# Two PSUM tiles in place of one two-bank tile for the transposes, and VectorE in place of GpSimd from attention slot 20

## The chip, the cores and the metric

The kernel runs on one core of one Trainium2 chip. The metric is the device time of one execution in microseconds (us); less is better. Five engines have instruction streams of their own: PE (TensorE), DVE (VectorE), ACT (ScalarE), POOL (GpSimd) and SP, which here only issues transfers. Each engine carries out its stream in order and waits on semaphores that other engines or transfers raise.

## The reference

One decoder layer on 512 tokens of width 1024, in float32:

```python
h = rmsnorm(x, g_mix_pre[i]);  z = h @ w_in[i]
(a_in, a_c, a_b, pv, cq, ck, cv, iq, ik, iw, dq, dk, dv) = jnp.split(z, split_at, axis=-1)
ya = short_conv_mixer(a_in, a_c, a_b, conv_w[i])
yb = pool_mixer(pv, pool_w[i], pool_scale[i])
yc = dsa_mixer(heads(cq), heads(ck), heads(cv), iq..., ik, iw, rel_bias[:DSA_HEADS])
yd = moba_mixer(heads(dq), heads(dk), heads(dv), rel_bias[DSA_HEADS:])
x = x + rmsnorm(jnp.concatenate([ya, yb, yc, yd], axis=-1) @ w_out[i], g_mix_post[i])
x = x + rmsnorm(swiglu(rmsnorm(x, g_ffn_pre[i]), w_gate_up[i], w_down[i]), g_ffn_post[i])
x = x + jax.nn.sigmoid(rmsnorm(x, g_ple[i]) @ w_ple_gate[i]) * (p[i] @ w_ple_proj[i])
```

The DSA mixer picks, for every query, the 128 keys of the highest index score and attends to these alone; the MoBA mixer attends to causal blocks. Both have four heads of width 64 and a relative-position bias.

## The kernel before

Everything is kept transposed, features on the 128 partitions and the 512 tokens along the free axis. Each float32 operand is split into a rounded high part and the low rest, and each product is made of three matmuls (`mm3`, lines 191 to 193): high times high, high times low, low times high. ScalarE makes the high part of a streamed weight chunk (`whi`, L172) and VectorE or GpSimd the low part (`wlo`, L176); the variable `lo_engine` says which.

The order of PE's work is written out by hand. A scheduler orders DVE, ACT, POOL and SP outside of the two stretches that are marked as manual. The stages are: projections and index scores (to about 85 us); attention, beside which DVE works off the top-k rounds until 161 us, and in which 16 MoBA and then 16 DSA items of 128 queries run through 36 slots (`attend`, L651) with projections and the output matrix as fill between them; the rest of the output matrix; a norm boundary (`boundary`, L844); the SwiGLU; a second boundary; and the last gate.

In slot s, `attend` issues the logits of item s into a PSUM tile `pss` (L436, L437; two of them in turn), the transposes of the probabilities of item s-3 (L624), their copy to SBUF as a high part by ACT (`hi`, L627) and a low part by DVE (`lo`, L628), and, when the item was the fourth of its head, the values product of that head (L640 to L644), which reads both parts of all four items. Before that, `prep` (L586) makes the bias `bs` of the item of slot s+1: for the DSA items the bias tile plus the selection mask, a two-input addition on GpSimd (L592). DVE reads a `pss` when it adds the bias and takes the maximum (L603); ACT then takes the exponential.

The transposes, the spreading of the norm's factors over the partitions (`Rms.spread`, L263), one of four product tiles in each boundary (`ple_steps`, L812) and one of the two tiles of each SwiGLU step come from `ptt` (L121). It hands out the two halves of one tile by turns:

```python
pair, turn = ps.tile([P, 2, T], F32, name="pair"), [0]
...
turn[0] += 1
return pair[:, turn[0] % 2]
```

Each half is one PSUM bank. In each boundary `spread` puts the factors into one half; DVE multiplies eight tiles by it (`mul`, L863), and `ple_steps` writes its fourth product into the other half.

In attention GpSimd has, besides `bs`, the low parts of the weights until slot 24, the low parts of the head outputs (`yd`, `yc`, L226 by L649) until slot 24, and three of the instructions of `conv_group` (L728) in both channel groups.

Of the kernel before, what the change touches and what calls it, by code (L numbers as in the profile page):

```python
# [9 lines left out]
F32 = mybir.dt.float32  # L10
F32R = mybir.dt.float32r
AF = mybir.ActivationFunctionType
OP = mybir.AluOpType
# [3 lines left out]
P = 128  # L17
T = 512
# [87 lines left out]
def tile_trunk(ctx: ExitStack, tc: tile.TileContext, xT, pT, sm, relx, wts, outT):  # L106
    nc = tc.nc
    G = ctx.enter_context(tc.tile_pool(name="glob", bufs=1))
    ps = ctx.enter_context(tc.tile_pool(name="ps", bufs=1, space=PSUM))
    dr = ctx.enter_context(tc.tile_pool(name="dr", bufs=1, space=DRAM))  # L110
    ctx.enter_context(tc.manual_schedule(engines={mybir.EngineType.PE}))

    pair, turn = ps.tile([P, 2, T], F32, name="pair"), [0]

    def pmm():
        return ps.tile([P, T], F32, tag="mm", bufs=4, name="pmm")

# [1 line left out]
        return ps.tile([P, T], F32, tag="s", bufs=2, name="pss")  # L119

    def ptt():  # L121
        turn[0] += 1
        return pair[:, turn[0] % 2]


    clock, put_off = [0], []
# [1 line left out]
    def later(n, fn, *args):  # L128
        put_off.append((clock[0] + n, fn, args))
# [14 lines left out]
    raws, wparts, sent, conv = [], {}, [0], [0]  # L144
    LOOK, RAW = 2, 3
    lo_engine = [nc.vector]
# [76 lines left out]
    def split(hi, lo, src, wait=0, eng=None):  # L223
        eng = eng or nc.vector
        nc.scalar.activation(hi, src, AF.Copy)
        f = lambda: eng.tensor_tensor(lo, src, hi.bitcast(F32), OP.subtract)  # L226
        later(wait, f) if wait else f()
# [8 lines left out]
    def col(name, i=0):  # L236
        a = _SM[name][0] + i
        return smt[:, a:a + 1]
# [3 lines left out]
    class Rms:  # L242
# [17 lines left out]
        def spread(self, copy=True):  # L260
            pb = self.rb = ptt()
            for j in range(NT):
                nc.tensor.transpose(pb[:, j * P:(j + 1) * P], self.r4[:, j:j + 1].to_broadcast([P, P]), ident)  # L263
            if copy:
                self.rb = G.tile([P, T], F32, tag="rb", bufs=1, name="rb")
                nc.scalar.activation(self.rb, pb, AF.Copy)
# [4 lines left out]
    def yslot(name, dt=F32R):  # L271
        return G.tile([P, T], dt, tag="y", bufs=8, name=name)
# [5 lines left out]
    with tc.tile_pool(name="mix", bufs=1) as M:  # L278
        def tmp(shape=(P, T), name="tmp", dt=F32):
            return M.tile(list(shape), dt, tag="tmp", bufs=8, name=name)  # L280
# [12 lines left out]
        zero = tmp(name="zero", dt=mybir.dt.bfloat16)  # L293
        nc.vector.memset(zero, 0.0)
        pz = ptt()
        for _ in range(WARM):
            nc.tensor.matmul(pz, zero[:, :P], zero, start=True, stop=True)
# [169 lines left out]
        def bias_vectors():  # L467
            vec = relt[:8, 8 + VECW:]
            parts = [(a, b, ptt()) for a, b in ((0, T), (T, VECW))]
            for a, b, pt in parts:  # L470
                nc.tensor.matmul(pt[:8, :b - a], relt[:, :8], relt[:, 8 + a:8 + b], start=True, stop=True)
            for a, b, pt in parts:
                nc.scalar.activation(vec[:, a:b], pt[:8, :b - a], AF.Copy)
            nc.gpsimd.dma_start(vec_1, vec)
            later(8, nc.gpsimd.dma_start, vec_d, vec_1[:, None, :].to_broadcast([8, P, VECW]))
# [42 lines left out]
        def rounds(n):  # L518
            for _ in range(n):
                next(tk, None)  # L520
# [41 lines left out]
        for j in range(NT):  # L562
# [4 lines left out]
                                           OP.mult, OP.subtract)  # L567
            V.append(v)

        y = [None] * KD  # L570
        PT, pts_used = [], [-1]

        class Attn:
# [12 lines left out]
            def prep(self, it):  # L586
                hh, i = it
                W = P * (i + 1)
                self.bs[it] = self.bm[hh][:, T - W:]
                if self.sel is not None and i > 0:  # L590
                    self.bs[it] = tmp((P, W), "bs")
                    nc.gpsimd.tensor_tensor(self.bs[it], self.bm[hh][:, T - W:], self.sel[i], OP.add)  # L592

            def logits(self, it):
                hh, i = it
# [34 lines left out]
            def values(self, hh):  # L630
                m, rows = hh // 2, slice(64 * (hh % 2), 64 * (hh % 2) + 64)
                if y[self.y0 + m] is None:
                    y[self.y0 + m] = (self.yalloc(), self.yalloc())
                pt = self.pt.pop(hh)
                o = pmm()
                for j in range(NT):
                    c = min(j * P, 256)
                    v = V[j][:, self.vcol + hh]
                    if j > 0:
                        nc.tensor.matmul(o[:64, c:], v[:, 0], pt[:, 1, j, c:], start=False, stop=False)  # L640
                    nc.tensor.matmul(o[:, c:], v.rearrange("p a c -> p (a c)"), pt[:, 0, j, c:], start=j == 0,
                                     stop=j == NT - 1)
                    if j == 0:
                        nc.tensor.matmul(o[:64, c:], v[:, 0], pt[:, 1, j, c:], start=False, stop=False)  # L644
                hi, lo = y[self.y0 + m]
                t = tmp(name="ol")
                nc.scalar.activation(t[rows], o[64:], AF.Copy)
                nc.vector.tensor_tensor(t[rows], o[:64], t[rows], OP.add)
                split(hi[rows], lo[rows], t[rows], 0, nc.gpsimd if slot[0] < 24 else nc.vector)  # L649

        def attend(items, fill, gaps, lag, ahead):  # L651

            def advance(n):
                for _ in range(n):
                    if next(fill, 0) == 0:
                        return
                    tick()
            n = len(items)
            for s in range(-ahead, n + lag + 1):
                if s + ahead < n:  # L660
                    at, it = items[s + ahead]
                    at.load_bias(it[0])
                    at.prep(it)
                if s < 0:
                    continue
                g = gaps(s)
                if s < n:
                    items[s][0].logits(items[s][1])
                advance(g[0])
                if 0 <= s - lag < n:  # L670
                    at, it = items[s - lag]
                    at.transpose(it)
                if s < n:
                    items[s][0].weights(items[s][1])
                advance(g[1])
                d = s - lag - 1
                if 0 <= d < n and items[d][1][1] == NT - 1:
                    items[d][0].values(items[d][1][0])
                advance(g[2])
# [4 lines left out]
        def keep(name):  # L684
            pt = pmm()
            yield from single(name, h, pt, K8)
            z = plain[name] = tmp(name=name)
            nc.vector.tensor_tensor(z, pt, r1.rb, OP.mult)
            if name[:2] == "pv":
                pool_sums(int(name[2]))  # L690
            if name[:3] == "a_b":
                conv_group(int(name[3]))
            yield
# [33 lines left out]

        def conv_group(m):  # L728
            a, c, b = (plain.pop(f"{n}{m}") for n in ("a_in", "a_c", "a_b"))
            nc.gpsimd.tensor_tensor(a, a, c, OP.mult)  # L730
            nc.gpsimd.tensor_scalar(c, a, col("conv", 3 * m + 2), 1.0, OP.mult, OP.mult)

            def taps():
                for s in (1, 2):
                    nc.vector.scalar_tensor_tensor(c[:, s:], a[:, :T - s], col("conv", 3 * m + 2 - s), c[:, s:],
                                                   OP.mult, OP.add)
                nc.gpsimd.tensor_tensor(c, c, b, OP.mult)
                y[m] = (yslot("yh"), yslot("yl"))
                later(3, split, y[m][0], y[m][1], c, 1)
            later(4, taps)  # L740
# [11 lines left out]
        wo, slot = [], [0]  # L752
# [7 lines left out]

        def gaps(s):
            slot[0] = s
            if s == 24:
                lo_engine[0] = nc.vector
            if s == 14:
                rounds(48)
            return GAPS[0] if s < 22 else GAPS[1] if s < 34 else GAPS[2]
        attend(items, fill, gaps, LAG, AHEAD)
        pt3 = pss()
        wo_n3 = single("wo_n3", y, pt3, WO_KS)  # L770
# [154 lines left out]
    with tc.tile_pool(name="ffn", bufs=1) as F:  # L925
# [60 lines left out]
        for n in range(KD):  # L986
# [10 lines left out]
            t = G.tile([P, T], F32, tag="h", bufs=16, name="fg")  # L997
# [101 lines left out]
```

## Time and profile before

| | us |
|---|---|
| median of three runs | 673.71 |
| the three runs | 672.12, 673.71, 675.39 |
| the profiled execution, its own time | 674.74 |
| its span, first to last instruction | 672.8 |

The page's first part gives the busy time of each engine within that span; DVE was busy for 61%, ACT for 42% and POOL for 12% of it. The mean granted clock of PE was 0.994 of full speed. The sections below go by the span's clock: 0 is the first instruction. A row of the timeline has the start, the duration, the engine, the line of the kernel, the operation, the tile written and the tiles read; in brackets stands how long the engine was idle before it and what ended that. The starts of back-to-back 512-column matmuls are 0.23 us apart, while each has a modelled duration of 0.39, since they overlap.

### The profile page before, as it was taken

To read this page: it belongs to the slowest core of one execution; us is meant where nothing else is said; L and a number is where in the kernel's file an instruction comes from. 1 tells how busy PE (TensorE), PEld (TensorE's weight loads), DVE (VectorE), ACT (ScalarE), POOL (GpSimd) and SP (SyncE) were. 2 spreads that over 40 slices of the span, in tenths; PEclk is the share of its full clock that TensorE was granted. 3 is DMA by queue.
4 is the path that set the end of the run, shared out by engine and by line. 5 is a ranking of instruction groups with operands and counts; after the bars stand their busy time and mean duration, and the time that the engine had idled before them with its cause. 6 is when DMAs were issued, how large, how long until landed. Compare 5 with 4: busy or idle time off the path is not lost.

```text
span 672.8 us, 8031 instructions
## 1 busy us (share of the span) xinstructions
PE 653.4 (97%) x2993; PEld 535.1 (80%) x2993; DVE 410.2 (61%) x707; ACT 285.2 (42%) x464; POOL 80.5 (12%) x82
## 2 busy tenths in 40 slices
PE   8999998999799989999999999999999999998997
PEld 6887887888577878888888888888888888887886
DVE  6869999998863547685554545455532222244867
ACT  7555265766674635342222222333322322333542
POOL 1110056375811000000000000000000000000000
PEclk9999999999989989999999999999999999999999
DMA  8457532524335413223323333323233323242303
GB/s 311 140 170 230 137 108 79 137 76 112 84 93 190 156 32 94 95 94 94 94 94 96 98 110 95 105 94 94 87 118 92 111 90 106 87 125 64 88 7 125
DMA packets 24774, 74.16 MB, mean 110 GB/s; under 512 B 3522, under 2 KB 3906, under 8 KB 24736
## 3 DMA queue, kind: packets, MB, share of 16 engines
q1 hardware_dynamic: 22656, 67.78, 32.4%
q0 software_dynamic: 2080, 5.88, 2.5%
q8 instruction: 23, 0.38, 0.2%
q14 instruction: 15, 0.12, 0.1%
HBM read 67.20 MB, written 4.74 MB: 107 GB/s over the span
## 4 chain that ended last, share of the span: by engine, by line
PE 79%; DVE 10%; issue 4%; DMA 3%; POOL 2%; ACT 1%; SPq 0%; DVEq 0%; POOLq 0%; ACTq 0%
PE pmm L191 10%; PE pmm L193 10%; PE pmm L192 10%; PE pss L193 7%; PE pss L192 6%; PE pss L191 6%; PE pair L191 6%; PE pair L192 6%; PE pair L193 6%; PE pmm L906 2%; PE pmm L910 2%; PE pmm L908 2%; PE pmm L328 2%; DVE acc L512 1%; DMA dq<-z 1%
## 5 line engine op out<-in xcount | busy, mean ns | idle before, releaser
L172 ACT ACTIVATE whi<-raw 128x1024 fp32r<-128x1024 f32 (+2 forms) x111 | 113.8, 1025 | 251.5 <-PE pmm L192 85.7
L176 DVE TENSOR_TENSOR wlo<-raw,whi 128x1024 fp32r<-128x1024 f32 (+2 forms) x99 | 120.7, 1219 | 103.1 <-ACT whi L172 103.0
L191 PE MATMUL pss<-hhi,whi 128*128 128x512 f32 (+1 forms) x184 | 72.0, 392 | 0.0
L193 PE MATMUL pss<-hhi,wlo 128*128 128x512 f32 (+1 forms) x184 | 71.8, 390 | 0.0
L192 PE MATMUL pss<-hlo,whi 128*128 128x512 f32 (+1 forms) x184 | 71.7, 390 | 0.0
L191 PE MATMUL pmm<-gth,whi 128*128 128x512 f32 x176 | 69.4, 394 | 0.0
L193 PE MATMUL pmm<-gth,wlo 128*128 128x512 f32 x176 | 69.0, 392 | 0.0
L192 PE MATMUL pmm<-gtl,whi 128*128 128x512 f32 x176 | 68.4, 388 | 0.0
L191 PE MATMUL pair<-hhi,whi 128*128 128x512 f32 x168 | 65.6, 390 | 0.0
L193 PE MATMUL pair<-hhi,wlo 128*128 128x512 f32 x168 | 65.5, 390 | 0.0
L192 PE MATMUL pair<-hlo,whi 128*128 128x512 f32 x168 | 65.4, 390 | 0.0
L191 PE MATMUL pmm<-hhi,whi 128*128 128x512 f32 (+1 forms) x144 | 56.8, 394 | 0.0
L192 PE MATMUL pmm<-hlo,whi 128*128 128x512 f32 (+1 forms) x144 | 54.8, 381 | 0.0
L193 PE MATMUL pmm<-hhi,wlo 128*128 128x512 f32 (+1 forms) x144 | 54.7, 380 | 0.0
L963 DVE TENSOR_TENSOR us<-pair,rb 128x512 f32<-128x512 f32 x19 | 13.1, 692 | 48.7 <-PE pair L193 48.7
L193 PEld LDWEIGHTS pss<-hhi,wlo 128*128 128x128 f32 (+1 forms) x184 | 34.2, 186 | 7.6
L192 PEld LDWEIGHTS pss<-hlo,whi 128*128 128x128 f32 (+1 forms) x184 | 34.2, 186 | 7.4
L191 PEld LDWEIGHTS pss<-hhi,whi 128*128 128x128 f32 (+1 forms) x184 | 34.2, 186 | 7.3
L193 PEld LDWEIGHTS pmm<-gth,wlo 128*128 128x128 f32 x176 | 33.0, 188 | 7.7
L192 PEld LDWEIGHTS pmm<-gtl,whi 128*128 128x128 f32 x176 | 33.1, 188 | 7.3
L191 PEld LDWEIGHTS pmm<-gth,whi 128*128 128x128 f32 x176 | 33.2, 188 | 6.6
L957 DVE TENSOR_TENSOR gs<-pss,rb 128x512 f32<-128x512 f32 x19 | 13.1, 691 | 40.2 <-PE pss L193 40.2
(266 smaller groups left out, 1214.7 us busy)
## 6 DMA issues: line engine op xcount, KB each, us to landing
raw<-in_wts_dram SPq DMA_DIRECT2D x98, 512.0 KB, 3.5
raw<-in_wts_dram SPq DMA_DIRECT2D x12, 384.0 KB, 3.0
vec_d<-vec POOLq DMA_DIRECT2D x1, 2560.0 KB, 20.7
xb<-in_xT_dram SPq DMA_DIRECT2D x8, 256.5 KB, 6.1
bm<-vec_d SPq DMA_DIRECT2D x8, 256.0 KB, 2.9
xr<-in_xT_dram POOLq DMA_DIRECT2D x8, 256.0 KB, 5.1
out_dram<-th SPq DMA_DIRECT2D x7, 256.0 KB, 2.0
klow<-klow SPq DMA_DIRECT2D x8, 128.0 KB, 3.5
```

What stands on the lines that cost most here:

```text
L172: nc.scalar.activation(hi, src, AF.Copy)
L176: lo_engine[0].tensor_tensor(lo, src, hi.bitcast(F32), OP.subtract)
L191: nc.tensor.matmul(out, a[0][sa], b[0][sb], start=start, stop=False)
L192: nc.tensor.matmul(out, a[0][sa], b[1][sb], start=False, stop=False)
L193: nc.tensor.matmul(out, a[1][sa], b[0][sb], start=False, stop=stop)
L328: nc.tensor.matmul(pts[n][:, P:], w[a][:, c[n]], h[k][b][:, P:], start=k + a + b == 0, stop=k == 7 and b == 1)
L512: nc.vector.match_replace(out=acc[i], in_to_replace=m8, in_values=acc[i], imm_value=TAKEN)
L906: nc.tensor.matmul(pts[n], w[0][:, c[n]], hs[k][0], start=k == 0, stop=False)
L908: nc.tensor.matmul(pts[n], w[1][:, c[n]], hs[k][0], start=False, stop=False)
L910: nc.tensor.matmul(pts[n], w[0][:, c[n]], hs[k][1], start=False, stop=k == KD - 1)
L957: nc.vector.tensor_tensor(gs, pg, rb, OP.mult)
L963: nc.vector.tensor_tensor(us, pu, rb, OP.mult)
```

## The change

`ptt` hands out tiles of its own, from a pool of two, in place of halves of one tile. A new function `helper` gives GpSimd in the slots below 20 and VectorE from then on; the bias addition, the low part of the head outputs, the three instructions of `conv_group` and the low parts of the weights go by it (the two low parts changed over at slot 24 before, the other two not at all).

```diff
-    pair, turn = ps.tile([P, 2, T], F32, name="pair"), [0]
     def ptt():
-        turn[0] += 1
-        return pair[:, turn[0] % 2]
+        return ps.tile([P, T], F32, tag="tt", bufs=2, name="ptt")
...
+        def helper():
+
+            return nc.gpsimd if slot[0] < 20 else nc.vector
...
-                    nc.gpsimd.tensor_tensor(self.bs[it], self.bm[hh][:, T - W:], self.sel[i], OP.add)
+                    helper().tensor_tensor(self.bs[it], self.bm[hh][:, T - W:], self.sel[i], OP.add)
...
-                split(hi[rows], lo[rows], t[rows], 0, nc.gpsimd if slot[0] < 24 else nc.vector)
+                split(hi[rows], lo[rows], t[rows], 0, helper())
...
-            nc.gpsimd.tensor_tensor(a, a, c, OP.mult)
-            nc.gpsimd.tensor_scalar(c, a, col("conv", 3 * m + 2), 1.0, OP.mult, OP.mult)
+            eng = helper()
+            eng.tensor_tensor(a, a, c, OP.mult)
+            eng.tensor_scalar(c, a, col("conv", 3 * m + 2), 1.0, OP.mult, OP.mult)
...
-                nc.gpsimd.tensor_tensor(c, c, b, OP.mult)
+                eng.tensor_tensor(c, c, b, OP.mult)
...
-            if s == 24:
-                lo_engine[0] = nc.vector
+            lo_engine[0] = helper()
```

How the streams of instructions change is shown at three places. A row is the line, the operation, the tile written, the tiles read and the size; in brackets stand the semaphores that the instruction waits on, by the engine that raises them. The changed kernel's lines are up to three lower or one higher.

On PE, in the first boundary, the last product into `pss` and the first into the tile of `ptt`; before:

```order
L191 MATMUL pss<-pp,klow_307 128x512
L192 MATMUL pss<-pp,klow_307 128x512
L193 MATMUL pss<-pp,klow_308 128x512
L191 MATMUL pair<-pp,klow_305 128x512 [waits DVE_49]
L192 MATMUL pair<-pp,klow_305 128x512
```

and changed:

```order
L188 MATMUL pss<-pp,klow_307 128x512
L189 MATMUL pss<-pp,klow_307 128x512
L190 MATMUL pss<-pp,klow_308 128x512
L188 MATMUL ptt<-pp,klow_305 128x512
L189 MATMUL ptt<-pp,klow_305 128x512
```

The wait on DVE is gone there; it is gone in the same way in the second boundary.

On PE, in attention, where the first DSA head ends: the transpose of the next head's first item, then the values product of the head; before:

```order
L193 MATMUL pmm<-hhi,wlo 128x512
L624 MATMUL pair<-smt,pr 128x128 [waits DVE_49]
L641 MATMUL pmm<-pt,v 128x512 [waits Activation_49]
L644 MATMUL pmm<-pt,v 64x512
L640 MATMUL pmm<-pt,v 64x384
```

and changed:

```order
L190 MATMUL pmm<-hhi,wlo 128x512
L625 MATMUL ptt<-smt,pr 128x128 [waits DVE_49,PE_49]
L642 MATMUL pmm<-pt,v 128x512 [waits Activation_49]
L645 MATMUL pmm<-pt,v 64x512 [waits DVE_49]
L641 MATMUL pmm<-pt,v 64x384
```

The second matmul of the values product, which reads the low part, has a wait on DVE of its own now; before, the wait of the transpose ahead of it covered it. The transpose's own wait on DVE is now for the reader of its own tile, two transposes back.

On DVE, at slot 20, from the last row of the top-k on; before:

```order
L514 TENSOR_SCALAR acc_384<-acc_384 128x512
L394 TENSOR_TENSOR z<-pmm,rb 128x512
L648 TENSOR_TENSOR ol<-pmm,ol 64x512
L603 ISA pr,st<-pss,bs 128x512
L603 ISA st 128x1
L603 ISA pr,st<-pss,bm 128x128
L603 ISA st 128x1
L426 TENSOR_TENSOR klow_308<-z,ck_1684 128x512
L628 TENSOR_TENSOR pt<-pair,pt 128x2x128
```

and changed:

```order
L511 TENSOR_SCALAR acc_385<-acc_385 128x512
L391 TENSOR_TENSOR z<-pmm,rb 128x512
L593 TENSOR_TENSOR bs<-bm,acc_384 128x384
L173 TENSOR_TENSOR wlo<-raw,whi 128x768
L649 TENSOR_TENSOR ol<-pmm,ol 64x512
L604 ISA pr,st<-pss,bs 128x512
L604 ISA st 128x1
L604 ISA pr,st<-pss,bm 128x128
L604 ISA st 128x1
L423 TENSOR_TENSOR klow_308<-z,ck_1703 128x512
```

Two of the moved instructions stand ahead of the head output `ol` and of the row L604 that reads `pss`. In all 14 instructions leave POOL for DVE between slots 20 and 31: eight `bs` (three of 128x512, three of 128x384, two of 128x256), two `wlo` of 128x768, one `yc`, and the three of the second `conv_group`. Three stay on POOL after the top-k's last row: `bs` of 128x512 and of 128x256, and the last `yd`. Ahead of slot 20 no instruction changes its place on any engine.

## Rows read from the trace of the kernel before

**Rows 1.** The page, part 1: busy us, share of span, instructions.
```profile
PE 653.4 (97%) x2993; PEld 535.1 (80%) x2993; DVE 410.2 (61%) x707; ACT 285.2 (42%) x464; POOL 80.5 (12%) x82
```

**Rows 2.** Waits of PE, whole span: us in total, times, longest us.
```profile
PE pair L624 <- DVE pt L628: 7.8, 8, 3.4
PE pair L191 <- DVE fg L863: 2.0, 1, 2.0
PE pair L191 <- DVE mg L863: 2.0, 1, 2.0
```

**Rows 3.** Timeline of PE and DVE, 103 to 113 us.
```profile
103.74 0.55 PE L624 MATMUL pair<-smt,pr 128*128 128x128 f32 x3 [0.82 <-DVE pt L628]
...
111.46 0.68 DVE L628 TENSOR_TENSOR pt<-pair,pt 128x512 fp32r<-128x512 f32 x1
112.19 0.33 PE L624 MATMUL pair<-smt,pr 128*128 128x128 f32 x1 [1.13 <-DVE pt L628]
```

**Rows 4.** Timeline of POOL, DVE and PE, 161 to 202 us.
```profile
161.52 2.98 POOL L592 TENSOR_TENSOR bs<-bm,acc 128x512 f32<-128x512 f32 x3 [5.39 <-DVE acc L514]
163.06 0.69 DVE L603 CUSTOM_DVE_ANT_0 pr<-pss,bs 128x512 f32<-128x512 f32 x1
163.89 1.16 DVE L426 TENSOR_TENSOR klow<-z,ck 128x512 fp32r<-128x512 f32 x1
164.09 0.28 PE L436 MATMUL pss<-ck,cq 128*128 128x256 f32 x1
166.84 1.29 POOL L226 TENSOR_TENSOR yd<-ol,yd 64x512 fp32r<-64x512 f32 x1
...
179.77 1.28 POOL L737 TENSOR_TENSOR a_c<-a_c,a_b 128x512 f32<-128x512 f32 x1
179.94 4.83 DVE L176 TENSOR_TENSOR wlo<-raw,whi 128x768 fp32r<-128x768 f32 x1
181.01 2.94 POOL L592 TENSOR_TENSOR bs<-bm,acc 128x256 f32<-128x256 f32 x3
181.71 0.40 PE L193 MATMUL pmm<-yh,wlo 128*128 128x512 f32 x1
185.49 0.33 PE L624 MATMUL pair<-smt,pr 128*128 128x128 f32 x1 [3.38 <-DVE pt L628]
185.90 0.40 PE L644 MATMUL pmm<-pt,v 128*64 128x512 f32 x1
...
200.40 0.96 DVE L176 TENSOR_TENSOR wlo<-raw,whi 128x768 fp32r<-128x768 f32 x1 [0.66 <-ACT whi L172]
```

**Rows 5.** Busy us by window: length, engines, then granted clock, DMA share, GB/s.
```profile
161.00:207.00 46.00, 39.95 (x197) 30.74 (x196) 32.42 (x72) 31.48 (x70) 25.78 (x27) 0.96 0.38 112
180.00:190.00 10.00, 6.62 (x28) 5.21 (x27) 8.28 (x14) 5.58 (x12) 3.95 (x4) 0.83 0.19 55
246.00:252.00 6.00, 4.45 (x13) 3.51 (x14) 3.87 (x7) 2.90 (x5) 0.00 (x0) 0.72 0.00 0
616.00:626.00 10.00, 8.00 (x37) 6.25 (x36) 8.01 (x12) 4.23 (x8) 0.00 (x0) 1.00 0.01 2
```

**Rows 6.** Timeline of PE and DVE in the first boundary, 245 to 251 us.
```profile
245.16 0.40 PE L193 MATMUL pss<-pp,klow 128*128 128x512 f32 x1
...
246.81 0.68 DVE L863 TENSOR_TENSOR mg<-mg,pair 128x512 f32<-128x512 f32 x1
...
247.55 0.63 PE L191 MATMUL pair<-pp,klow 128*128 128x512 f32 x1 [2.00 <-DVE mg L863]
...
250.97 0.69 DVE L863 TENSOR_TENSOR mg<-mg,pair 128x512 f32<-128x512 f32 x1 [2.09 <-ACT pph L820]
```

**Rows 7.** Groups of DVE by line and shape: count, then busy us, mean ns.
```profile
L868 DVE TENSOR_TENSOR x<-mg,xr 128x512 f32<-128x512 f32 x8 | 5.5, 690 | 0.2
L628 DVE TENSOR_TENSOR pt<-pair,pt 128x384 fp32r<-128x384 f32 x8 | 4.4, 548 | 1.2 <-ACT pt L627 1.2
L628 DVE TENSOR_TENSOR pt<-pair,pt 128x256 fp32r<-128x256 f32 x8 | 3.3, 410 | 0.0
```

## The prediction

> **What bounds the kernel now.** I read the page's busy times first, then PE's waits, then the timeline around each of them, and last the windows with the granted clock. PE is busy 97% of the span [rows 1], so only time in which PE waits, or runs slower than it could, is to be had; a shorter DVE or POOL instruction is worth what it takes off a wait of PE. PE's waits are few [rows 2]: 7.8 us in eight waits of the attention's transposes for the low-part copy L628 on DVE, the longest 3.4, and 2.0 us in each boundary, where a product into `pair` waits for a multiplication L863 on DVE. Both are waits on `pair`. In the boundary the multiplication reads one half and the product writes the other, and the first place of the change's order drops this wait without a substitute: it came from the two halves being one tile. In attention the transposes write the half that the copy before does not touch; there it is the same, but the values product needs that copy anyway.
>
> The third loss is the clock. Granted clock was 0.83 in 180 to 190 us and 0.72 in 246 to 252 [rows 5], that is half speed (1.2 in place of 2.4 GHz) for a part of each window, right behind the waits of 3.38 and of 2.00 us [rows 4, 6]. Lost are 0.17 x 10 = 1.7 us in each place, as 0.28 x 6 = 1.7. The second boundary's wait, also 2.0 us [rows 2], cost no clock: 1.00 in 616 to 626 [rows 5].
>
> **The boundaries.** Nothing is added. In the first, the last matmul into `pss` starts at 245.16 and the next one at 247.55, idle 2.00 [rows 6]; it waits for the multiplication that runs from 246.81 to 247.49. Its operands, the same chunk as the matmuls ahead, are there. So 2.0 us go. What would be late next: after this product come the first matmuls of the SwiGLU's weights, whose operand is made by DVE and ACT. DVE loses a wait as well: its multiplication at 250.97 had been idle for 2.09 us on account of `pair`, behind ACT's copy of that product [rows 6]. DVE thus comes forward by about as much as PE, and I see no new wait. With the wait goes the half speed behind it, 1.7 us. The first boundary gives 3.7, the second 2.0.
>
> **Attention before slot 20.** Here only the tile changes; DVE's order is the same, and the top-k keeps DVE busy. PE waited 0.82 us at 103.74 and 1.13 at 112.19 [rows 3]. The first is for the false dependence alone and goes. But then PE comes to the second 0.82 earlier, and that one is the place ahead of a values product: its second matmul needs the same copy, which ends at 111.46 + 0.68 = 112.14 whatever PE does. PE can do only the transpose and the first matmul of the product under the wait, 185.90 - 185.49 = 0.4 us at the like place [rows 4]. Sum here: 0.4 us, not 1.95.
>
> **Attention from slot 20.** What can be had at most: PE is busy 39.95 of 46.00 us from 161 to 207 [rows 5], so 6.05 idle, and the clock's 1.7: 7.8 us. The largest piece, the 3.38, has its cause on DVE: the copy that PE waited for stood behind a weight's low part that ran from 179.94 for 4.83 us, while the same shape takes 0.96 at 200.40 [rows 4]. In just that time POOL ran four two-input instructions back to back, 179.77 to 183.95; the DVE instruction ended 0.82 after the last of them [rows 4]. I take it that DVE was held until POOL was done. The Trainium skill (SBUF — State Buffer, Who interferes with whom) says that a DVE instruction with two SBUF inputs and a GpSimd one exclude each other, the second blocking until the first has finished. By that DVE would have gone on when the first of POOL's four ended, at 181.05, 2.9 us sooner than POOL's last; with 2.9 of another origin left in place the sum below would be 6.6. The trace shows the longer hold, and the sum goes by the trace.
>
> The change takes all POOL work out of that place. The 14 instructions cost DVE, by the nearest DVE rows: eight `bs`, 3 x 0.69 + 3 x 0.55 + 2 x 0.41 = 4.5 [rows 7]; two `wlo` at 0.96 [rows 4]; `yc` and two of the convolution's at 0.69, the third, with one input, unseen there and put between 0.41 and 0.69, at 0.4 [rows 7]. Together 8.9 us. The long instruction gives back 4.83 - 0.96 = 3.9. DVE has 46.0 - 32.4 = 13.6 us idle there [rows 5], so it holds 5 more; it does not become the bound over the stretch. But it works in order, and at slot 20 it is a queue. There lie the new waits:
>
> First, two moved instructions stand ahead of `ol` and of the maximum L603 that frees a `pss` for PE. That row ended at 163.06 + 0.69 = 163.75, and PE's next logits started at 164.09 [rows 4], so there was 0.3 us of slack. Now the `bs` and the `wlo` (0.55 + 0.96) come first, and POOL, which runs its last two `bs` from 161.52 on, can hold each of them: I get about 164.9 for their end, then `ol` and the maximum, 166.1. PE, 0.4 early, wants the tile at 163.7: a new wait of 2.2 to 2.4 us. Second, the key's low part behind it already took 1.16 beside POOL, and now meets the last `yd` of 1.29 [rows 4], so DVE is some 3 us behind; its idle time lets it catch up only in part by the first values product, which I see waiting 1.2. At the product that waited 3.38 I get 0.8, and 0.2 at the last. New waits: 2.2 + 1.2 + 0.8 + 0.2 = 4.4. Net 7.8 - 4.4 = 3.4 us. Bounds of this term: 7.8 if nothing new waits, nothing if the new waits eat all.
>
> **Sum.** 0.4 + 3.4 + 3.7 + 2.0 = 9.5 us. Against the profiled execution's 674.74 that is 665.2; it lay 1.0 above the median of 673.71, against which it is 664.2. I forecast 664.2. What lies behind attention apart from the boundaries, the SwiGLU above all, has no wait of PE [rows 2] and moves forward as it is.
>
> **Rivals.**
> 1. The queue at slot 20 drains faster: POOL does not hold DVE, and the scheduler's order fits. For it: 13.6 us of idle DVE [rows 5]. Against: the 4.83 [rows 4]. Then 0.4 + 7.8 + 5.7 = 13.9, so 659.8. Chance 0.2.
> 2. Attention gives nothing, since DVE's added work is waited for as long as POOL's was, or the new wait of 2.2 us at slot 20 costs 1.7 of clock as that of 2.00 did [rows 5, 6]. The boundaries remain, 5.7: 668.0. A like price comes from the clock alone: one wait of 2.0 cost it and another did not [rows 2, 5], so another run of the kernel before may lack the 1.7 that I count in the first boundary. And if POOL held the long DVE instruction only until the first of its four ended, 181.05, then 2.9 of the wait stays: 9.5 - 2.9 = 6.6, so 667.1. The Trainium skill (TensorE: Matmul & The Clock Gate, What's actually happening) has it that the clock is judged at moments that do not follow the kernel, and that the count of slow matmuls differs from run to run; by this, 1.7 of my 9.5 is there in some runs only. Chance of all these together 0.2.
> 3. Slower: each of nine slots from 20 on has a moved instruction ahead of the row that frees PE's `pss`, as at slot 20. If all nine wait the 2.2 us of the first, 19.8 stand against 13.9, 5.9 more than before: 679.6. It decides from 13.9 / 9 = 1.5 us a slot. Against it: only the first slot meets the end of the top-k and POOL's rest, and the 13.6 idle lies behind it. Chance 0.04.
> 4. The change doesn't do what it says: the new tiles bring waits for the release of a tile in place of the old ones, and the long DVE instruction was not POOL's doing. Then within 2 us of 673. The order speaks against the first half, and POOL's rows against the second [rows 4]. Chance 0.06.
>
> **How the numbers follow.** My forecast has 0.5. Rival 1 sets the low end, 659.5; the high end, 668.5, takes in rival 2; outside lie rivals 3 and 4. A measurement of this kernel tells 0.5%, 3.4 us, from no change. Faster by more is all of the forecast and rivals 1 and 2, 0.90; within it rival 4, 0.06; slower rival 3, 0.04.
>
> **What would show it.** Right: no wait of PE on the tile of `ptt` in the boundaries, clock 1.00 in the first; no DVE `wlo` of 128x768 much above 1 us after slot 20; POOL without arithmetic from about 168 us until the boundary; waits left at the logits of slot 20 and at values products, on DVE's L604 and L629. Wrong: PE waiting in the boundaries on something else, a wait of some 2 us at most slots from 20 on, or the product in the stretch of the 3.38 still waiting over 2 us.

## The result, and the profile after

| | before | after |
|---|---|---|
| median, us | 673.75 (4 runs) | 665.75 (4 runs) |
| lowest and highest run, us | 672.12, 675.39 | 665.26, 667.30 |
| the profiled execution, us | 674.74 | 665.27 |
| its span, us | 672.8 | 663.4 |

The ratio of the times is 0.9881, with a 95% interval of 0.9852 to 0.9909: faster by 1.2%. The sum of the prediction, 665.2 against the profiled execution, stands beside 665.27; its 664.2 against the median stands beside 665.75.

The page's first part, as [rows 1]:

```profile
PE 650.4 (98%) x2993; PEld 534.3 (81%) x2993; DVE 413.2 (62%) x721; ACT 284.1 (43%) x464; POOL 64.1 (10%) x68
```

The waits of PE over the span, as [rows 2] (us in total, times, longest). None is left on the tile of `ptt` in attention or in the boundaries; the largest two are new:

```profile
PE pss L433 <- DVE st L604: 2.9, 1, 2.9
PE pmm L645 <- DVE pt L629: 2.8, 4, 1.2
```

The first of them, in the timeline of DVE, POOL and PE, 160 to 168 us, to be read beside the first rows of [rows 4]. VectorE ends the top-k at 160.94, then has the two moved instructions ahead of `ol` and of L604, and both take longer than alone, since GpSimd has its last two `bs`; behind them, the key's low part meets `yd`:

```profile
160.51 0.43 DVE L511 TENSOR_SCALAR acc<-acc 128x512 f32<-128x512 f32 x1
160.85 0.68 DVE L391 TENSOR_TENSOR z<-pmm,rb 128x512 f32<-128x512 f32 x1
161.01 2.32 POOL L593 TENSOR_TENSOR bs<-bm,acc 128x512 f32<-128x512 f32 x2 [5.39 <-DVE acc L511]
161.45 1.28 DVE L593 TENSOR_TENSOR bs<-bm,acc 128x384 f32<-128x384 f32 x1
162.66 1.49 DVE L173 TENSOR_TENSOR wlo<-raw,whi 128x768 fp32r<-128x768 f32 x1
...
164.90 0.69 DVE L604 CUSTOM_DVE_ANT_0 pr<-pss,bs 128x512 f32<-128x512 f32 x1
...
165.65 0.39 PE L433 MATMUL pss<-ck,cq 128*128 128x256 f32 x1 [2.89 <-DVE st L604]
165.66 1.27 POOL L223 TENSOR_TENSOR yd<-ol,yd 64x512 fp32r<-64x512 f32 x1 [2.33 <-ACT yd L222]
165.72 1.76 DVE L423 TENSOR_TENSOR klow<-z,ck 128x512 fp32r<-128x512 f32 x1
```

(These logits, which the prediction calls those of slot 20, are by count the item of slot 21; the moved instructions ahead of them are issued in slot 20.) The wait cost clock as well, as the windows show (columns as in [rows 5]); the half speed of 180 to 190 us and that of the first boundary are gone:

```profile
166.00:170.00 4.00, 4.00 (x15) 3.17 (x14) 2.46 (x7) 2.64 (x10) 0.94 (x1) 0.58 0.54 164
180.00:190.00 10.00, 9.29 (x51) 7.51 (x50) 9.82 (x28) 7.84 (x21) 0.00 (x0) 1.00 0.17 54
240.00:252.00 12.00, 12.00 (x54) 9.63 (x53) 11.83 (x18) 7.15 (x12) 0.00 (x0) 1.00 0.13 44
```

In the first boundary (timeline of PE, beside [rows 6]) the first product into the tile of `ptt` follows the last into `pss` by 0.23 us, where it came 2.39 later before:

```profile
241.53 0.39 PE L190 MATMUL pss<-pp,klow 128*128 128x512 f32 x1
241.76 0.40 PE L188 MATMUL ptt<-pp,klow 128*128 128x512 f32 x1
```

**Where the time went.** The starts of four matmuls on PE cut the span into stretches: the logits of the items of slots 1 and 20, the first product of the fourth output tile behind attention, and the last matmul. What lies ahead of the first of them is not in the table. The same cuts serve for the kernels of the experiments below (one profiled execution each, us):

| kernel | slot 1 to 20 | 20 to the end of attention | from there to the last |
|---|---|---|---|
| before | 72.34 | 46.34 | 460.60 |
| after | 71.01 | 44.24 | 454.84 |
| the tiles alone | 71.09 | 45.93 | 454.92 |
| the engines alone | 72.41 | 46.73 | 459.08 |
| one instruction moved (`yc`) | 71.10 | 42.01 | 454.85 |
| two moved | 71.02 | 40.06 | 454.84 |
| two moved, one tile | 72.46 | 42.14 | 459.04 |
| bias and convolution on GpSimd | 71.11 | 41.21 | 454.91 |
| all from slot 21 | 71.01 | 40.33 | 454.84 |

After against before: 1.33, 2.10 and 5.76 us; 0.2 more lies ahead of slot 1.

### The profile page after: what moved, and what is told of

It is laid out like the page before. It is cut to its first block, busy times and chain, and to the rows that moved or that the text cites. A ratio compares the mean times of both kernels' runs of the same rounds, so it can differ in the third digit from the quotient of the medians.

```text
span 663.4 us, 8008 instructions
## 1 busy us (share of the span) xinstructions
PE 650.4 (98%) x2993; PEld 534.3 (81%) x2993; DVE 413.2 (62%) x721; ACT 284.1 (43%) x464; POOL 64.1 (10%) x68
## 4 chain that ended last, share of the span: by engine, by line
PE 83%; DVE 12%; DMA 2%; issue 1%; ACT 1%; SPq 0%; DVEq 0%; ACTq 0%
PE pmm L188 11%; PE pmm L190 11%; PE pmm L189 11%; PE pss L190 7%; PE pss L188 7%; PE pss L189 7%; PE ptt L188 6%; PE ptt L190 6%; PE ptt L189 6%; DVE acc L509 2%; PE pmm L907 2%; PE pmm L911 2%; PE pmm L909 2%; PE pmm L325 2%; DVE m L508 2%; DMA dq<-z 1%
## 5 line engine op out<-in xcount | busy, mean ns | idle before, releaser
L173 DVE TENSOR_TENSOR wlo<-raw,whi 128x1024 fp32r<-128x1024 f32 (+2 forms) x101 | 119.3, 1181 | 100.9 <-ACT whi L169 100.8
L188 PE MATMUL ptt<-hhi,whi 128*128 128x512 f32 x168 | 65.6, 390 | 0.0
L190 PE MATMUL ptt<-hhi,wlo 128*128 128x512 f32 x168 | 65.4, 389 | 0.0
L189 PE MATMUL ptt<-hlo,whi 128*128 128x512 f32 x168 | 65.4, 389 | 0.0
L964 DVE TENSOR_TENSOR us<-ptt,rb 128x512 f32<-128x512 f32 x19 | 13.1, 692 | 49.0 <-PE ptt L190 49.0
```

The costliest lines, as they stand in the source:

```text
L173: lo_engine[0].tensor_tensor(lo, src, hi.bitcast(F32), OP.subtract)
L188: nc.tensor.matmul(out, a[0][sa], b[0][sb], start=start, stop=False)
L189: nc.tensor.matmul(out, a[0][sa], b[1][sb], start=False, stop=False)
L190: nc.tensor.matmul(out, a[1][sa], b[0][sb], start=False, stop=stop)
```

## The experiments

**The two halves of the change.** The kernel before with this alone:

```diff
-    pair, turn = ps.tile([P, 2, T], F32, name="pair"), [0]
-        turn[0] += 1
-        return pair[:, turn[0] % 2]
+        return ps.tile([P, T], F32, tag="tt", bufs=2, name="ptt")
```

> The kernel before with the two tiles alone; all work stays on GpSimd as before. My account: the boundaries give what they gave in the full change (about 3.4 and 2.1 us) and attention little (0.4), because the values product needs the low-part copy that the transposes waited for: about 5.9 us less than before, 667.8 us, and a wait of about 3 us is left at the values product near 185 us, behind the same long low part of a weight on VectorE. Rival: the false dependence itself was attention's loss, so the tiles alone give all 8.0: 665.7 us, and no wait above 1 us near 185.

Measured: 667.94 us median of 6 (before, on the same chip, 674.67 of 17), ratio 0.9911 [0.9886, 0.9935]. The first account holds for the time. The wait near 185 us is larger than it said, though, 4.92 (timeline of PE, DVE and POOL; behind it the clock's row, columns as in [rows 5]):

```profile
177.38 1.29 POOL L223 TENSOR_TENSOR yc<-ol,yc 64x512 fp32r<-64x512 f32 x1 [1.89 <-ACT yc L222]
178.64 1.30 POOL L589 TENSOR_TENSOR bs<-bm,acc 128x512 f32<-128x512 f32 x1
...
179.73 5.09 DVE L173 TENSOR_TENSOR wlo<-raw,whi 128x768 fp32r<-128x768 f32 x1
179.90 1.26 POOL L734 TENSOR_TENSOR a_c<-a_c,a_b 128x512 f32<-128x512 f32 x1
...
180.73 0.50 PE L638 MATMUL pmm<-pt,v 128*128 128x512 f32 x1 [0.47 <-ACT pt L624]
181.12 2.88 POOL L589 TENSOR_TENSOR bs<-bm,acc 128x256 f32<-128x256 f32 x3
...
184.82 0.66 DVE L600 CUSTOM_DVE_ANT_0 pr<-pss,bs 128x512 f32<-128x512 f32 x1
...
185.42 0.68 DVE L625 TENSOR_TENSOR pt<-ptt,pt 128x512 fp32r<-128x512 f32 x1
186.15 0.69 PE L641 MATMUL pmm<-pt,v 128*64 128x512 f32 x1 [4.92 <-DVE pt L625]
...
180.00:190.00 10.00, 4.61 (x15) 3.49 (x16) 7.14 (x9) 3.99 (x10) 4.01 (x4) 0.66 0.19 55
```

and in the kernel before, at the same place:

```profile
177.26 1.29 POOL L226 TENSOR_TENSOR yc<-ol,yc 64x512 fp32r<-64x512 f32 x1 [1.88 <-ACT yc L225]
178.51 1.29 POOL L592 TENSOR_TENSOR bs<-bm,acc 128x512 f32<-128x512 f32 x1
...
184.77 0.67 DVE L628 TENSOR_TENSOR pt<-pair,pt 128x512 fp32r<-128x512 f32 x1
```

VectorE's long instruction ends at 184.82, where it ended at 184.77 before. The wait is 1.54 longer because PE is ready for it at 181.23, 0.88 earlier than the 182.11 of [rows 4], and because VectorE's next row is now L600 and the copy comes 0.65 later. The clock lost 0.34 x 10 = 3.4 us behind it, twice what it lost here before [rows 5].

GpSimd's run is six instructions long in both kernels: the low part `yc` over 64 partitions, a 128x512 addition, the product, and three additions. VectorE asked while GpSimd was in the second of them, in the kernel before in the third, and got its turn when the sixth ended, at 184.00: its own end lies 0.82 behind that, as it did behind the sixth, at 183.95, in the kernel before [rows 4].

Then the full change with the one tile kept:

```diff
+    pair, turn = ps.tile([P, 2, T], F32, name="pair"), [0]
-        return ps.tile([P, T], F32, tag="tt", bufs=2, name="ptt")
+        turn[0] += 1
+        return pair[:, turn[0] % 2]
```

> The full change with the one two-bank tile kept; the work from slot 20 is on VectorE. My account: attention gives about 3.2 of the 3.6 us, both boundaries keep their waits of 2.0 us, and the first may keep the half clock behind it: 669.5 to 671.5 us. Rival: the engine move does nothing without the two tiles, since the transposes still wait for copies that are now queued behind more work: 673 or more.

Measured: 675.13 us (12 runs), ratio 1.0011 [0.9993, 1.0029]. My account was wrong and the rival right: by itself the move gives nothing. PE's waits show why:

```profile
PE pair L628 <- DVE pt L632: 7.4, 9, 1.3
PE pair L191 <- DVE mg L867: 2.0, 1, 2.0
PE pair L191 <- DVE fg L867: 2.0, 1, 2.0
PE pss L436 <- DVE st L607: 1.9, 1, 1.9
```

The eight waits of 7.8 us for the copy [rows 2] became nine of 7.4, none as long as 3.38: with one tile a transpose waits for the copy of the other half. I take it that the copies came later because VectorE had more to do (busy 36.6 us of the 46 of [rows 5], 32.4 before); no run separates that. The two parts of the change are thus not a sum. The tiles give 6.0 to 6.7 alone, the engines nothing alone and about 2 on top of the tiles.

**Which of the fourteen moved instructions matter.** The two that stood ahead of L604 go back to GpSimd:

```diff
-            return nc.gpsimd if slot[0] < 20 else nc.vector
+            return nc.gpsimd if slot[0] < 21 else nc.vector
```

> The full change with helper() at slot 21 in place of 20: exactly two instructions go back to GpSimd, the bias of 128x384 and the weight's low part of 128x768 that stood ahead of the row that frees the logits' tile. My account: the wait of 2.89 us at the logits of slot 20 falls to 0.3 or less, and with it the half clock behind it, 1.7 us; GpSimd runs 3 us longer beside the key's low part, so 0.5 to 1.5 us come back at the first values product: 662 to 663.5 us. Rival 1: the wait belongs to the end of the top-k at 160.5 us and not to the two instructions: 665.7 us, wait unchanged. Rival 2: the half clock does not hang on this wait: wait gone, 663, with a stretch of half clock elsewhere.

Measured: 662.01 us, ratio 0.9820 [0.9793, 0.9847], as expected. The wait of 2.89 is 0.4, and no stretch of half clock is left: 0.999 over the span. These two instructions cost the change 3.7 us. With slot 22 in place of 21:

> The full change with helper() at slot 22: one more bias addition (128x512) goes back to GpSimd than with slot 21. My account: with the queue at slot 20 gone already, this addition lies where VectorE has idle time, so nothing changes: 661.5 to 662.5 us, no wait above 1.3 us. Rival: GpSimd's longer tail holds VectorE at the first values product: 663 or more with a wait of 1 to 2 us there.

Measured: 661.82 us (5 runs), ratio 0.9818 [0.9794, 0.9843]: the same; no wait on VectorE in attention is over 1.1.

Next, 11 of the 14 stay on GpSimd:

```diff
-                    helper().tensor_tensor(self.bs[it], self.bm[hh][:, T - W:], self.sel[i], OP.add)
+                    nc.gpsimd.tensor_tensor(self.bs[it], self.bm[hh][:, T - W:], self.sel[i], OP.add)
-            eng = helper()
+            eng = nc.gpsimd
```

> The full change with the bias additions and the three instructions of the convolution left on GpSimd throughout (11 of the 14 moved ones); only the two low parts of weights and the one of a head output go to VectorE at slot 20. My account: GpSimd's runs of two-input instructions come back, and with them VectorE instructions of 3 us or more between slots 22 and 27 and a wait of 2 to 3.4 us of TensorE at a values product; the wait at slot 20 shrinks to about 1.5; about 667.5 us (between 666.5 and 669). Rival: GpSimd's additions harm nothing, and the long VectorE instruction of the kernel before came from the two low parts of weights on GpSimd: no VectorE instruction above 2 us behind slot 21, 664 to 665 us.

Measured: 662.98 us, ratio 0.9837 [0.9809, 0.9864]. My account was wrong, the rival right and more as far as the time goes (the cause that it names, the weights' low parts, is for the next run): with those 11 on GpSimd the kernel is 2.8 us faster than the full change. The wait at slot 20 is 1.9, with no loss of clock. So the additions alone did not make the long hold. What remains moved are two low parts of weights and `yc`. The last one alone, against the kernel with the tiles alone:

```diff
-                split(hi[rows], lo[rows], t[rows], 0, nc.gpsimd if slot[0] < 24 else nc.vector)
+                split(hi[rows], lo[rows], t[rows], 0, helper())
```

> The two tiles, and a single instruction moved: the low part of the first DSA head's output goes to VectorE. My account: what makes the hold of 5 us is that GpSimd runs without a pause from that low part on (it waits for ScalarE first, then has five instructions ready behind it); without it GpSimd pauses before the convolution's product and VectorE's low part gets in after one instruction: no VectorE instruction above 2 us there, 661.5 to 664 us. Rival: the hold is made by the bias additions in a row or by the amount of work on GpSimd, and stays: 667 to 668.5 us, a wait of 4 to 5 us at the values product.

Measured: 662.98 us (4 runs), ratio 0.9834 [0.9808, 0.9860]. One instruction of 14, added to the tiles, gives 5.0 us, more than all 14 (2.2). The timeline of POOL, DVE and PE shows the hold gone:

```profile
178.68 1.28 POOL L739 TENSOR_TENSOR a_c<-a_c,a_b 128x512 f32<-128x512 f32 x1 [1.81 <-DVE a_b L689]
...
179.39 1.39 DVE L173 TENSOR_TENSOR wlo<-raw,whi 128x768 fp32r<-128x768 f32 x1
179.92 4.12 POOL L593 TENSOR_TENSOR bs<-bm,acc 128x256 f32<-128x256 f32 x3
...
182.10 0.69 PE L645 MATMUL pmm<-pt,v 128*64 128x512 f32 x1 [1.21 <-DVE pt L629]
```

The same product and the same three additions as above, and VectorE gets in when the product ends; the additions wait instead (4.12 for 2.88). With `yc` gone GpSimd also pauses ahead of the product, so this run alone doesn't tell which of the two ended the hold. Yet 180 to 190 us has a clock of 0.83 here, behind no wait longer than 1.21 (one of 0.47 stands 1.2 us ahead of that); two of the four executions had a mean clock of 0.999, so it is not in each of them. The same with the second low part of a weight moved too (helper at slot 21, bias and convolution on GpSimd):

> The two tiles, and only two of the fourteen instructions moved to VectorE: the second low part of a weight and the low part of the first DSA head (the switch of these two at slot 21; bias additions and convolution stay on GpSimd throughout). My account: nothing is ahead of the row that frees the logits' tile at slot 20, so no wait there (1.9 us with the first low part moved as well); and GpSimd's run at the convolution starts after an idle stretch and lets VectorE's low part in after one instruction, so that takes 1.0 to 1.5 us: 660.5 to 662 us, the lowest so far. Rival: the hold of 5 us for the low part comes back, since GpSimd has as many additions there as in the kernel with the tiles alone: 666 to 668 us.

Measured: **661.32 us**, 661.12 to 661.72 in four runs, ratio 0.9809 [0.9784, 0.9834]: the lowest median of all, and clear of the full change's interval; the runs from slot 22 (661.69 to 662.45) touch it. In 161 to 207 us PE is busy 44.20 of 46.00 us at full clock (39.95 at 0.96 in [rows 5]; attention ends at 199.36 here, so the last 7.6 us of the window lie behind it):

```profile
161.00:207.00 46.00, 44.20 (x224) 35.26 (x223) 31.90 (x75) 31.38 (x71) 25.08 (x25) 1.00 0.46 149
```

And that kernel with the one tile:

> The kernel with two moved instructions (second low part of a weight, low part of the first DSA head), but with the one two-bank tile of the kernel before. It tells what the two tiles are worth once VectorE's long hold is gone. My account: in attention the transposes wait for the low-part copies of the other half again, which cost 7.4 us in nine waits when the engines alone were changed; some 4 of these come back, with 4.0 us of waits in the boundaries: 668 to 671 us. Rival: without the hold the false dependence costs only the boundaries' 4.0 us and attention nothing: 665 to 666 us.

Measured: 670.74 us (8 runs), ratio 0.9949 [0.9930, 0.9967]; 5.2 us in seven waits for the copy are back in attention:

```profile
PE pair L628 <- DVE pt L632: 5.2, 7, 1.5
```

By the table of stretches the two tiles are worth 1.44 + 2.08 + 4.20 = 7.7 us there; the two medians, from different chips, lie 9.4 apart.

**What holds VectorE.** Two theories were left: GpSimd keeps VectorE out as long as it has instructions ready, or something in that run does it. Three kernels that hold nothing of the layer measured it by itself.

> A kernel of its own that computes nothing of the layer: 24 times, GpSimd runs five two-input additions of 128x512 in a row (third group: 512, 512, 256, 384, 512 wide) while VectorE, after 0 to 7 small fills that set its start, runs one two-input subtraction of 128x768. Eight times without waits between GpSimd's five, eight times each of them waiting for the one before, eight times with the mixed sizes. Account A (VectorE gets in at GpSimd's next instruction boundary): VectorE's instruction takes at most 1.3 + 0.9 = 2.2 us in all 24. Account B (GpSimd keeps the memory as long as it has instructions ready): 3 to 6.5 us without waits between, short with waits between. Account C (it depends on the moment at which VectorE asks): both kinds within one group, by the number of fills.

Measured: 0.89 to 1.69 us in all 24, so account A. Five ready instructions in a row do not hold.

> A kernel of its own that computes nothing of the layer and repeats the run of six GpSimd instructions that stood beside the long hold (64x512 into fp32r, 128x512, a product in place, 256, 384, 512 wide), with VectorE's 128x384 PSUM copy, then its 128x768 low part, then a row that reads PSUM, and ScalarE copies beside; ten starting points of VectorE each, in four groups: all of it; without the 64x512; the product not in place; without the PSUM copy. Account A (some property of that run makes the hold): VectorE's low part takes 3 us or more at some starting points of the first group, and not in the group that lacks the property. Account B (neither the shapes nor the order make it, but something else of the layer's kernel): at most 2.2 us in all 40.

Measured: 2.51 to 3.67 us at 11 of the 30 starting points in the three groups with the 64x512 instruction; at most 1.94 at all ten of the group without it; at most 2.00 elsewhere. Account A, with the 64x512 (or the length of the run) as the property.

The core of the last (written on fewer lines here), in which the number `r` of fills sets VectorE's start and `kind` is the group:

```python
for q in range(r):
    nc.vector.memset(z[:, 128 + 32 * q:384 + 32 * q], 0.0)
nc.vector.tensor_tensor(pt[:, :384], pp[:, :384], x[:, :384], sub)
nc.vector.tensor_tensor(wlo, raw, whi, sub)
...
if kind == 0: nc.gpsimd.tensor_tensor(yf, ol, x, sub)
elif kind == 1: nc.gpsimd.tensor_tensor(yf[:64], ol[:64], x[:64], sub)
elif kind == 2: nc.gpsimd.tensor_tensor(yc, ol, x, sub)
nc.gpsimd.tensor_tensor(bs[0], bm, acc, add)
nc.gpsimd.tensor_tensor(a_c, a_c, a_b, OP.mult)
if kind == 3: nc.gpsimd.tensor_tensor(yc[:64], ol[:64], x[:64], sub)
...
```

> The second probe again, which showed holds of 2.5 to 3.7 us in the three groups whose run of GpSimd began with the 64x512 instruction and none in the group without it; but those runs were also six instructions long and the other five. Ten starting points each: six with a 128x512 into float32 first; six with a 64x512 into float32 first; six with a 128x512 into fp32r first; six with the 64x512 into fp32r in the third place; and eight of 128x512 without any 64x512. Account A (the instruction over 64 partitions makes the hold): long holds in the second and fourth group alone. Account B (the length of the run makes it: six or more ready in a row): long holds in all five groups, the longest in the last. Account C (the fp32r output): third and fourth group.

Measured: the second and the fourth group have four holds each, 3.67, 3.28, 2.89 and 2.50; the other three none above 2.03, the run of eight included. Account A. The same start of VectorE, first with a 128x512 at the head of the run, then with a 64x512 (timeline of POOL and DVE; the last row is the one that gave way):

```profile
57.23 1.26 POOL L152 TENSOR_TENSOR yf<-ol,x 128x512 f32<-128x512 f32 x1
...
59.67 1.26 POOL L158 TENSOR_TENSOR a_c<-a_c,a_b 128x512 f32<-128x512 f32 x1
59.76 1.99 DVE L147 TENSOR_TENSOR wlo<-raw,whi 128x768 fp32r<-128x768 f32 x1
...
134.85 1.26 POOL L154 TENSOR_TENSOR yf<-ol,x 64x512 f32<-64x512 f32 x1
...
137.28 1.26 POOL L158 TENSOR_TENSOR a_c<-a_c,a_b 128x512 f32<-128x512 f32 x1
137.38 3.67 DVE L147 TENSOR_TENSOR wlo<-raw,whi 128x768 fp32r<-128x768 f32 x1
138.50 0.72 POOL L163 TENSOR_TENSOR bs<-bm,acc 128x256 f32<-128x256 f32 x1
139.18 0.99 POOL L163 TENSOR_TENSOR bs<-bm,acc 128x384 f32<-128x384 f32 x1
140.13 2.04 POOL L163 TENSOR_TENSOR bs<-bm,acc 128x512 f32<-128x512 f32 x1
```

Last, in the layer: the tiles alone, with `yc` on GpSimd over 128 partitions.

```diff
+                wide = slice(0, P) if self.sel is not None and hh == 0 else rows
+                if wide != rows:
+                    nc.vector.memset(t[64:], 0.0)
...
-                split(hi[rows], lo[rows], t[rows], 0, nc.gpsimd if slot[0] < 24 else nc.vector)
+                split(hi[wide], lo[wide], t[wide], 0, nc.gpsimd if slot[0] < 24 else nc.vector)
```

> The kernel with the tiles alone (all work on GpSimd as before), with one change of form: the low part of the first DSA head's output on GpSimd runs over all 128 partitions in place of 64 (the other 64 are zeros, written by VectorE ahead, and overwritten by the next head). The order of GpSimd's run is the same: this one, 128x512, a product, 256, 384, 512. Account A (as the last probe had it, an instruction over 64 partitions in GpSimd's run makes the hold): VectorE's low part of 128x768 takes 1.0 to 2.0 us in place of 5.09, no wait above 1.5 us at the values product: 661.5 to 664 us. Account B (in the layer it is the length of the run): the hold of some 5 us stays, 667.5 to 668.5 us.

Measured: 663.48 us (5 runs), ratio 0.9825 [0.9802, 0.9849]; the low part takes 1.77. That is the time of account A, but the run did not isolate the cause (ScalarE's high part of `yc` is over 128 partitions too, and VectorE has the filling of the zeros):

```profile
174.54 1.32 POOL L223 TENSOR_TENSOR yc<-ol,yc 128x512 fp32r<-128x512 f32 x1
174.63 3.05 DVE L735 SCALAR_TENSOR_TENSOR a_c<-a_in,smt,a_c 128x511 f32<-128x511 f32 x1 [0.29 <-POOL a_c L731]
...
179.89 1.27 POOL L737 TENSOR_TENSOR a_c<-a_c,a_b 128x512 f32<-128x512 f32 x1 [2.76 <-DVE st L606]
...
180.20 1.77 DVE L173 TENSOR_TENSOR wlo<-raw,whi 128x768 fp32r<-128x768 f32 x1
```

GpSimd came to `yc` earlier, and then paused for 2.76 us ahead of the product, so the run was not the old one; and a convolution tap of VectorE took 3.05 us (0.74 the second time) past the end of `yc`, with no 64-partition instruction in GpSimd's run since 167.79. The width is thus shown as a cause in the probes; in the layer the hold goes when `yc` leaves, and went in the one run with `yc` widened, whose order of events changed with it; and something else can make a shorter one. The clock of 180 to 190 us was 0.83 in this run as well, behind two waits of 1.27 and 1.25.

## Why the prediction was right, step by step

**The boundaries** (3.7 + 2.0) are right in size and in cause: 5.76 us by the third stretch. With the tiles and no engine moved it is 454.92, with the engines and no tiles 459.08; the 4.2 between is the two waits. The other 1.5 (460.60 against 459.08, both with one tile) is the first boundary's clock, which the profiled execution lost and others need not: the kernel with the engines alone waits 1.99 there at clock 1.00. Rival 2 had this. 47 runs of the kernel before were timed beside the experiments, and their mean clock runs from 0.991 (675.87 to 676.54 us) to 0.999 (671.66 to 673.25, nine runs). The Trainium skill (TensorE: Matmul & The Clock Gate, What's actually happening) has the slow matmuls differ from run to run; these runs agree. A mean clock of 0.999 leaves at most 0.0015 x 671 = 1.0 us of loss, so those nine lost neither the 1.7 of this boundary nor the 1.7 that the prediction counts behind the 3.38. Both terms are thus of some executions only.

**Attention before slot 20** was put at 0.4 and gave 1.33. The step that failed is "PE can do only the transpose and the first matmul of the product under the wait", taken from the like place at 185 us. At 112 us the program has another product between the two (three matmuls), so that 1.1 us of work went under the wait and not 0.4: in the kernel after, the first matmul that needs the copy starts at 111.99, where it started at 113.30 before, behind a wait of 1.16 for a copy that ended 0.2 earlier than before, as everything does there:

```profile
111.26 0.68 DVE L629 TENSOR_TENSOR pt<-ptt,pt 128x512 fp32r<-128x512 f32 x1
...
111.99 0.45 PE L645 MATMUL pmm<-pt,v 128*64 128x512 f32 x1 [1.16 <-DVE pt L629]
```

**Attention from slot 20** was put at 7.8 - 4.4 = 3.4 and gave 2.10. Of the 7.8, at least 6.3 can be had: two moved instructions bring this stretch to 40.06. The queue at slot 20 was seen in its place; its term was mis-sized, 2.89 in place of 2.2 to 2.4, and it cost the 1.7 of clock that rival 2 had: 0.42 x 4 = 1.7 in 166 to 170. VectorE's maximum, forecast to end at 166.1, ended at 164.90 + 0.69 = 165.59; the wait is longer because PE was there at 162.76 and not at the 163.7 of the forecast. On the other side the products waited 0.72 and 0.71 where 1.2 and 0.8 were expected. So 0.9 too little before slot 20 and 1.3 too much after made a sum that fits. The 0.9 is one error that stands in both terms: VectorE frees that tile when it does, and what PE gains ahead of it only lengthens the wait. What is left is luck: the clock's 1.7, which the sum did not have, against waits that VectorE ended sooner than forecast.

**The cause of the 3.38** was half right. VectorE was held by GpSimd, as taken; but the run that held it was two instructions longer than the four that the prediction read, and `yc` was the first of the two. And "the change takes all POOL work out of that place" is not why it went: with 11 of the 14 left there it goes too, and it goes when the one 64x512 leaves. The Trainium skill (SBUF — State Buffer, Who interferes with whom) has VectorE wait for one GpSimd instruction; 95 of the probes' 114 starts agree, the 19 long ones and the rows of this kernel do not. The three that matter are the tiles, `yc` and the second low part; the other 12 moved instructions cost 4.4 us (665.75 against 661.32), and 3.7 of it lies in two of them at slot 20 (665.75 against 662.01); the 0.7 of the other ten is near the noise.

**The other rivals.** Rival 1's time, 659.8, is what a schedule without the queue comes near to (661.3). Rival 3's nine waits did not come: one of 2.89 and none above 1.2. Of rival 4 the waits for a release did not come, and the probes show that VectorE is held by GpSimd.

## What to carry to other kernels

Look for one tile that holds two banks before moving any work: here its false waits hid the whole gain of the move, and the two gains did not add up. Where an engine is to be relieved, find the single instruction whose start or shape makes the long stall, and move that; each further one is a place in a queue that somebody waits on, worst here where VectorE had just ended its top-k. And where a like place is used to price a wait, read the program between the two instructions in both places.

## What the runs showed of the hardware

- A VectorE instruction with two SBUF inputs, 0.89 to 0.97 us at its least, got in at once or at the end of GpSimd's current instruction in 95 of 114 starts; where it had to wait, its end lay 0.81 to 0.88 us behind the end that let it in. With a two-input GpSimd instruction over 64 partitions in a run of six, at the first or the third place, a VectorE that asked in the third or fourth instruction got in only at the end of the fifth (19 times, 2.5 to 3.7 us; one that asked 0.07 us into the third got in at once). In the layer, asking in the third and in the second, it got in only at the end of the sixth (4.83 and 5.09 us). What sets the end that lets it in was not settled.
- The float32 or fp32r output of that instruction made no difference (3.67, 3.28, 2.89 and 2.50 us with either).
- In the profiled executions half clock came behind waits of 2.89, 3.38 and 4.92 us, behind one of 2.0 in one execution and not in another, and twice behind two shorter waits close together (0.47 and 1.21; 1.27 and 1.25), but behind neither a single wait of 1.9 nor one of 1.15. The nine runs of the kernel before at 0.999 show that it need not come behind 3.38 either.
